# Half of the second MLP product by Strassen's seven block products, interleaved with the first product

## The chip, the cores and the metric

The kernel runs on one core of one Trainium2 chip. Its time is the device time of one execution in microseconds, the median of several runs. A core has five engines that work through queues of their own and wait for each other by semaphores: TensorE (PE; its weight loads are listed as PEld), VectorE (DVE), ScalarE (ACT), GpSimd (POOL) and SyncE (SP, which here issues the loads of weights). The order in each queue is fixed when the program is built.

## The reference

One decoder layer on 256 tokens with 2048 features, all float32. Two token mixers (attention and a gated recurrence) come first; the part that matters here is the MLP at the end:

```
x = x + merged @ w_out
u = relu(rmsnorm(x) * g @ w_mlp1)      # w_mlp1: 2048 x 8192
return x + (u * u) @ w_mlp2            # w_mlp2: 8192 x 2048
```

## The kernel before, in words

Weights stream from HBM in tiles ("units") of 128 x 2048 float32, 1 MB each, 258 of them. Each is cut into two parts: ACT copies it to `hi` in the rounded type float32r, DVE subtracts to get the rest, `lo` = raw - hi. A product is then the sum of three: hi x hi, lo x hi, hi x lo. `unit()` hands out the next unit and, before it does, issues the load and the cut of the unit two further on; raw, `hi` and `lo` have three buffers each.

The MLP runs in four parts. A part makes 2048 of the 8192 hidden features and then adds what they contribute to the output:

- First product, 16 units of `w1` (`ws`, L288 and L290): features on partitions, 256 tokens in the columns. Each unit takes 16 matmuls of 512 columns (`hi` of the weight against both parts of x2) and 16 of 256 columns. Its result leaves PSUM in two pieces (`cross` on ACT, then an addition on DVE), goes through relu and the norm on DVE, is squared on ACT, and is cut into the parts of `ucat`, 128 x 256 each.
- Second product, 16 units of `w2` (L666 to L668): for each block b of 512 output columns, two PSUM banks (t = 0, 1, the two halves of the tokens) take 4 units. A unit is 4 rows of k by 2 values of t by 3 matmuls of 512 columns: 24. After the fourth unit the banks are copied by ACT (part 0) or added by DVE into `acc` (L674, L676).

At the end `turn` transposes the sums on PE, adds them to x2 and stores. x2 stays in SBUF from the layer's middle to the end. PSUM has eight banks, four in the pool `pmain` and four in `pside`. The scheduler that orders the queues keeps nearly the order of the code but moves instructions of one engine past each other where they don't depend.

The lines of the profile that follow: L116 makes `hi`, L117 makes `lo`, L301 `cross`, L302 the addition, L650 the relu with the norm, L652 the square, L314 and L315 the two parts of `ucat`, L612 the last addition into x2.

Of the kernel before, what the change touches and what calls it, by code (L numbers as in the profile page):

```python
# [9 lines left out]
F32 = mybir.dt.float32  # L10
# [6 lines left out]
P = 128  # L17
T = 256
# [12 lines left out]
def layer_kernel(ctx: ExitStack, tc: tile.TileContext, xT, vecs, wv, wm, wg, wu, wo, w1, w2, cf, cm, out):  # L31
# [3 lines left out]
    wp = ctx.enter_context(tc.tile_pool(name="weights", bufs=3))  # L35
    catp = ctx.enter_context(tc.tile_pool(name="cat", bufs=1))
    gp = ctx.enter_context(tc.tile_pool(name="gen", bufs=20))
    sp = ctx.enter_context(tc.tile_pool(name="small", bufs=3))
# [9 lines left out]
    def g4(s, shape=(P, 1024), dt=F32):  # L48
        return gp.tile(list(shape), dt, tag="g", name=uid(s))

    def s1(s, dt=F32, n=256):
        return sp.tile([P, n], dt, tag=f"s{n}", name=uid(s), bufs=6 if n == 256 else 3)

    def bank(s, pool=pp):
        return pool.tile([P, 512], F32, tag="b", name=uid(s))
# [13 lines left out]
    for p in range(4):  # L69
        for u in range(16):  # L70
            units.append(w1[16 * p + u])
        for b in range(4):
            at = 32 * (p // 2) + 8 * b
            w = w2[at : at + 8].rearrange("(u s) p f -> s p u f", s=2)[p % 2]
            for q in range(4):
                units.append(w[:, :, q * 512 : (q + 1) * 512])
# [9 lines left out]
    def load(u):  # L86
        if u >= len(units) or u in raws:
            return
        raws[u] = wp.tile([P, UW], F32, tag="raw", name=f"raw{u}")
        for s in pieces(u):  # L90
            if u < 4:
                load_x(u, s)
            if len(units[u].shape) == 2:
                nc.sync.dma_start(raws[u][:, s], units[u][:, s])
            else:
                nc.sync.dma_start(raws[u].rearrange("p (u f) -> p u f", u=4), units[u])
# [9 lines left out]

    def cut(u):
        if u >= len(units):
            return
        hi = wp.tile([P, UW], F32R, tag="hi", name=f"hi{u}")  # L110
        lo = wp.tile([P, UW], F32R, tag="lo", name=f"lo{u}")
        raw = raws[u]
# [8 lines left out]
    done = [0]  # L121

    def unit():
        u = done[0]
        done[0] += 1
        load(u + AHEAD)
        cut(u + AHEAD)
        return split.pop(u)
# [26 lines left out]
    warm = gp.tile([P, 512], F32R, tag="g", name="warm")  # L155
# [8 lines left out]
    cft = cp.tile([P, 128 + 256], F32, name="cft")  # L164
    rope = cp.tile([32, 512], F32, name="rope")
# [3 lines left out]
    def load_consts():  # L169
        nc.sync.dma_start(cft, cf[:, :384])  # L170
# [7 lines left out]
    ident = cft[:, :128]  # L178
    cmask = cft[:, 128:384]
# [36 lines left out]
    def prepare():  # L216
# [12 lines left out]
        ssum = cp.tile([P, T], F32, name="ssum")  # L229
# [93 lines left out]
    def recur(g, q, f):  # L323
# [36 lines left out]
        for lv in range(LEVELS):  # L360
# [3 lines left out]
            if lv < 7:  # L364
# [44 lines left out]
                nt = sp.tile([P, n], F32, tag="tot" if n > 256 else "tots", name=uid("tot"), bufs=2)  # L409
# [63 lines left out]
    def rotate(x):  # L473
        r = gp.tile([32, 4, T], F32, tag="g", name=uid("rot"))
# [7 lines left out]
    def attend(g, q, k):  # L482
# [8 lines left out]
        nmx = sp.tile([P, 8], F32, tag="c8", name=uid("nmx"), bufs=8)  # L491
        sm = sp.tile([P, 8], F32, tag="c8", name=uid("sm"), bufs=8)
# [107 lines left out]

    x2 = []
# [5 lines left out]
    acc2 = s1("acc2")  # L607
# [15 lines left out]
    rstd2 = cp.tile([P, T], F32, name="rstd2")  # L623


    x2cats = [x2cat[:, k, :] for k in range(KD)]
    acc = [[g4("acc", (P, 1024)) for _ in range(2)] for _ in range(2)]

    def turn(b):

        for j in range(4):
            ptr = bank("pt")
            for t in range(2):
                a = acc[t][b // 2][:, (b % 2) * 512 + j * P : (b % 2) * 512 + (j + 1) * P]
                nc.tensor.transpose(ptr[:, t * P : (t + 1) * P], a, ident)  # L635
            d = x2[b][:, j, :]
            nc.vector.tensor_add(d, ptr[:, :T], d)
            (nc.scalar if j % 2 else nc.sync).dma_start(out[4 * b + j], d)

    for part in range(4):  # L640
        ucat = []
        for j in range(16):
            pst = ws(unit_parts(*unit(), x2cats))
            if part == 0 and j == 0:
                ps2 = bank("ps_ss2")
                nc.tensor.matmul(ps2[:, :T], ones, acc2, start=True, stop=True)
                rms_rows(ps2[:, :T], rstd2, D)
            t = s1("t")
            summed(pst, t)
            nc.vector.scalar_tensor_tensor(t, t, 0.0, rstd2, op0=OP.max, op1=OP.mult)  # L650
            u2 = s1("u2")
            nc.scalar.activation(u2, t, AF.Square)  # L652
            if j % 2 == 0:
                ut = g4("ucat", (P, 2, 512), F32R)
            to_parts((ut[:, j % 2, :T], ut[:, j % 2, T:]), u2)
            ucat.append(ut[:, j % 2, :])
        for b in range(4):
            pst = [bank(f"py{t}", pm) for t in range(2)]
            for q in range(4):
                hi, lo = (w.rearrange("p (u k f) -> p k u f", u=4, k=4) for w in unit())  # L660
                for k in range(4):
                    kk = 4 * q + k
                    for t in range(2):
                        uh = ucat[kk][:, t * P : (t + 1) * P]
                        ul = ucat[kk][:, T + t * P : T + (t + 1) * P]
                        nc.tensor.matmul(pst[t], uh, hi[:, k], start=(kk == 0), stop=False)  # L666
                        nc.tensor.matmul(pst[t], uh, lo[:, k], start=False, stop=False)  # L667
                        nc.tensor.matmul(pst[t], ul, hi[:, k], start=False, stop=(kk == 15))  # L668
                if part == 3 and q == 0 and b > 0:
                    turn(b - 1)  # L670
            for t in range(2):
                d = acc[t][b // 2][:, (b % 2) * 512 : (b % 2 + 1) * 512]
                if part == 0:
                    nc.scalar.activation(d, pst[t], AF.Copy)  # L674
                else:
                    nc.vector.tensor_add(d, pst[t], d)  # L676
    turn(3)


# [84 lines left out]
```

## Time and profile before

| | us |
|---|---|
| median of 3 runs (lowest, highest) | 1431.89 (1430.42, 1432.04) |
| the profiled execution | 1432.35 |
| its span | 1430.6 |
| the MLP in it | about 718 to 1424 |

| engine | busy us | share |
|---|---|---|
| PE | 1423.7 | 100% |
| PEld | 1231.1 | 86% |
| DVE | 873.0 | 61% |
| ACT | 697.2 | 49% |

The busy time of PE is modelled from matmuls that overlap, so the spacing of matmuls is read from their starts. A mean over the span hides that the stages load DVE and ACT differently; the windows by stage show that.

### The profile page before, as it was taken

Reading aid. Unit: us, or ns where it says so; the run is one execution under the profiler, and the core shown is the slowest. Engines: PE = TensorE matmul, PEld = TensorE weight load, DVE = VectorE, ACT = ScalarE, POOL = GpSimd, SP = SyncE. Lnnn points to the kernel's source line nnn. Section 1 sums busy time; section 2 is a strip of 40 time slices with the busy share of each in tenths; the row PEclk is TensorE's granted clock in tenths of the full one; section 3 lists DMA queues with packets and bytes.
Section 4 is the critical chain, followed back from the end, with each engine's and each line's share of the span. In section 5 each row is a group of like instructions: output and inputs, shape, how many; then the busy total and the mean of one; then the engine's idle time right before and its main releaser. Section 6 shows DMA issues by size and latency. Waiting matters only on the chain.

```text
span 1430.6 us, 19881 instructions
## 1 busy us (share of the span) xinstructions
PE 1423.7 (100%) x8400; PEld 1231.1 (86%) x8400; DVE 873.0 (61%) x956; ACT 697.2 (49%) x794; POOL 4.9 (0%) x12
## 2 busy tenths in 40 slices
PE   9999999999999999999999999999999999999998
PEld 7888888888888888888888888888888888888887
DVE  7445776667876676666666534565546654566553
ACT  7444444676655555544454443554334543344431
POOL 0000000000000000000000000000000000000000
PEclk9999999999999999999999999999999999999999
DMA  8655544444443555555455565555665556555671
GB/s 302 226 200 193 177 158 160 156 177 177 177 147 148 193 205 208 204 194 203 178 192 190 178 188 196 204 182 183 194 204 191 194 177 193 190 206 180 185 222 61
DMA packets 67081, 267.99 MB, mean 187 GB/s; under 512 B 5648, under 2 KB 7824, under 8 KB 44208
## 3 DMA queue, kind: packets, MB, share of 16 engines
q1 hardware_dynamic: 65120, 263.53, 53.4%
q0 software_dynamic: 576, 2.10, 0.4%
q8 instruction: 66, 1.08, 0.3%
q10 hardware_dynamic: 1296, 1.09, 0.2%
q14 instruction: 23, 0.19, 0.0%
HBM read 264.60 MB, written 2.10 MB: 186 GB/s over the span
## 4 chain that ended last, share of the span: by engine, by line
PE 99%; DMA 0%; DVE 0%; ACT 0%; issue 0%; DVEq 0%
PE pw L288 43%; PE pw L290 22%; PE py L667 8%; PE py L666 8%; PE py L668 8%; PE pv L271 2%; PE pv L272 2%; PE pv L273 2%; PE pd L373 0%; PE pl L504 0%; DMA vt<-vecs 0%; PE pt L635 0%; PE pd L380 0%; PE pb L448 0%; PE pb L449 0%; PE ptr L526 0%
## 5 line engine op out<-in xcount | busy, mean ns | idle before, releaser
L117 DVE TENSOR_TENSOR lo<-raw,hi 128x2048 fp32r<-128x2048 f32 (+2 forms) x258 | 569.0, 2207 | 454.9 <-ACT hi L116 453.4
L116 ACT ACTIVATE hi<-raw 128x2048 fp32r<-128x2048 f32 (+2 forms) x258 | 475.5, 1845 | 444.0 <-PE pw L288 200.2
L288 PE MATMUL pw<-xcat,hi 128*128 128x512 f32 x1152 | 278.1, 393 | 0.0
L288 PEld LDWEIGHTS pw<-xcat,hi 128*128 128x128 f32 x1152 | 212.0, 188 | 42.2
L288 PE MATMUL pw<-x2cat,hi 128*128 128x512 f32 x1024 | 244.4, 391 | 0.0
L288 PEld LDWEIGHTS pw<-x2cat,hi 128*128 128x128 f32 x1024 | 188.5, 188 | 36.8 <-DVE x2cat L614 0.2
L666 PE MATMUL py<-hi,ucat 128*128 128x512 f32 x512 | 199.5, 390 | 0.0
L667 PE MATMUL py<-lo,ucat 128*128 128x512 f32 x512 | 199.2, 389 | 0.0
L668 PE MATMUL py<-hi,ucat 128*128 128x512 f32 x512 | 199.2, 389 | 0.0
L290 PEld LDWEIGHTS pw<-xcat,lo 128*128 128x128 f32 x1152 | 147.7, 191 | 5.6
L290 PE MATMUL pw<-xcat,lo 128*128 128x256 f32 x1152 | 149.4, 283 | 0.0
L290 PEld LDWEIGHTS pw<-x2cat,lo 128*128 128x128 f32 x1024 | 131.3, 191 | 4.9
L290 PE MATMUL pw<-x2cat,lo 128*128 128x256 f32 x1024 | 132.8, 283 | 0.0
L668 PEld LDWEIGHTS py<-hi,ucat 128*128 128x128 f32 x512 | 96.1, 188 | 20.0
L666 PEld LDWEIGHTS py<-hi,ucat 128*128 128x128 f32 x512 | 96.2, 188 | 19.8
L667 PEld LDWEIGHTS py<-lo,ucat 128*128 128x128 f32 x512 | 96.2, 188 | 19.6
L652 ACT ACTIVATE u<-t 128x256 f32<-128x256 f32 x64 | 26.4, 412 | 131.6 <-DVE t L650 131.6
L301 ACT ACTIVATE cross<-pw 128x256 f32<-128x256 f32 x168 | 62.2, 371 | 35.9 <-PE pw L290 35.8
L288 PE MATMUL pw<-mcat,hi 128*128 128x512 f32 x256 | 61.2, 391 | 0.0
L288 PEld LDWEIGHTS pw<-mcat,hi 128*128 128x128 f32 x256 | 47.0, 188 | 9.4 <-DVE mcat L315 0.3
L271 PE MATMUL pv<-hi,xcat 128*128 128x512 f32 x128 | 50.1, 399 | 1.2 <-ACT xcat L200 1.2
L272 PE MATMUL pv<-lo,xcat 128*128 128x512 f32 x128 | 50.5, 395 | 0.0
(172 smaller groups left out, 994.3 us busy)
## 6 DMA issues: line engine op xcount, KB each, us to landing
raw<-w SPq DMA_DIRECT2D x128, 1024.0 KB, 5.5
raw<-wm SPq DMA_DIRECT2D x56, 1024.0 KB, 4.8
raw<-wg SPq DMA_DIRECT2D x16, 1024.0 KB, 4.8
raw<-wu SPq DMA_DIRECT2D x16, 1024.0 KB, 4.8
raw<-wo SPq DMA_DIRECT2D x16, 1024.0 KB, 4.8
raw<-wv SPq DMA_DIRECT2D x10, 1024.0 KB, 4.9
raw<-wv SPq DMA_DIRECT2D x8, 512.0 KB, 7.2
raw<-wv SPq DMA_DIRECT2D x8, 256.0 KB, 5.5
```

Source lines behind the costliest of these rows:

```text
L116: nc.scalar.activation(hi[:, s], raw[:, s], AF.Copy)
L117: nc.vector.tensor_sub(lo[:, s], raw[:, s], hi[:, s].bitcast(F32))
L271: nc.tensor.matmul(pst[t], xh, hi[:, k, :], start=(kk == 0), stop=False)
L272: nc.tensor.matmul(pst[t], xh, lo[:, k, :], start=False, stop=False)
L273: nc.tensor.matmul(pst[t], xl, hi[:, k, :], start=False, stop=(kk == KD - 1))
L288: nc.tensor.matmul(pst, h, cat, start=(i == 0), stop=False)
L290: nc.tensor.matmul(pst[:, T:], l, cat[:, :T], start=False, stop=(i == n - 1))
L301: nc.scalar.activation(c, pst[:, T:], AF.Copy)
L652: nc.scalar.activation(u2, t, AF.Square)
L666: nc.tensor.matmul(pst[t], uh, hi[:, k], start=(kk == 0), stop=False)
L667: nc.tensor.matmul(pst[t], uh, lo[:, k], start=False, stop=False)
L668: nc.tensor.matmul(pst[t], ul, hi[:, k], start=False, stop=(kk == 15))
```

## The change

The hidden features are now taken in eight eighths of 1024. For the output columns of b = 0 and 1, a pair of values of t and the two halves of an eighth form 2 x 2 blocks, and seven of the eight eighths compute them by Strassen's scheme in Winograd's form: seven block products instead of eight, each 4 x 3 matmuls of 512 columns. The columns of b = 2 and 3 stay plain and gather in four PSUM banks (`slow`) over all eighths. Each of the seven products is added into its own SBUF tile (`fast`), and `combine` forms the four blocks once at the end. The sums of u (`side_sums`) and the differences of weights (`p_t1` to `p_t4`) are made on DVE. While an eighth's second product runs, the first product of the next one runs in between, in the order of a string of 19 letters: f a unit of the first product, s one of the seven, p a plain unit. The last eighth is done plainly. x2 is written to HBM before the MLP and read back at the end, and the pools of the early stages are closed and replaced.

```diff
+    dp = ctx.enter_context(tc.tile_pool(name="spill", bufs=1, space=bass.MemoryType.DRAM))
...
+    early = ExitStack()
+    pool = {
+        "g": early.enter_context(tc.tile_pool(name="gen", bufs=20)),
+        "s": early.enter_context(tc.tile_pool(name="small", bufs=3)),
+    }
...
+    def rows(k, b):
+        half, s, q = k // 8, k // 4 % 2, k % 4
+        at = 32 * half + 8 * b
+        w = w2[at : at + 8].rearrange("(u s) p f -> s p u f", s=2)[s]
+        return w[:, :, q * 512 : (q + 1) * 512]
...
+    def ahead(u):
+        if u < MLP:
+            load(u)
+            cut(u)
+        elif u - MLP < len(later):
+            split[u] = later[u - MLP][0]()
...
+    slow = [[bank(f"py{b}{t}") for t in range(2)] for b in range(2)]
...
+    def raw_of(name, src):
+        if name[0] == "w":
+            r = wp.tile([P, UW], F32, tag="raw", name=uid(name))
+        else:
+            r = pool["s"].tile([P, UW], F32, tag="raw2", name=uid(name), bufs=2)
+        if len(src.shape) == 2:
+            nc.sync.dma_start(r, src)
+        else:
+            nc.sync.dma_start(r.rearrange("p (u f) -> p u f", u=4), src)
+        return r
...
+    def halves(r):
+        hi, lo = two_parts(uid("w"))
+        nc.scalar.activation(hi, r, AF.Copy)
+        nc.vector.tensor_sub(lo, r, hi.bitcast(F32))
+        return hi, lo
...
+            if j == 0:
+                ucat[c] = []
+                usum[c] = [g4("uk", (P, 4, T)) for _ in range(2)]
+            pst = ws(unit_parts(*unit(), x2cats))
...
+            if j == 7 and c + 1 < EIGHTHS:
+                side_sums(c)
...
+    def side_sums(c):
+        (a1, a2), H = usum.pop(c), slice(0, P)
+        L = slice(P, T)
+        nc.vector.tensor_add(a2[:, :, L], a1[:, :, L], a2[:, :, L])
+        nc.vector.tensor_sub(a1[:, :, L], a1[:, :, H], a1[:, :, L])
+        nc.vector.tensor_sub(a1[:, :, H], a2[:, :, L], a1[:, :, H])
+        nc.vector.tensor_sub(a2[:, :, H], a2[:, :, H], a1[:, :, H])
+        parts = []
+        for a in (a1, a2):
+            h, l = (g4(n, (P, 4, T), F32R) for n in ("sh", "sl"))
+            to_parts((h, l), a)
+            parts.append((h, l))
+        upart[c] = parts
...
+    def rows_product(pst, stat, parts, begin, end):
+        hi, lo = (w.rearrange("p (u k f) -> p k u f", u=4, k=4) for w in parts)
+        for k, (xh, xl) in enumerate(stat):
+            nc.tensor.matmul(pst, xh, hi[:, k], start=(begin and k == 0), stop=False)
+            nc.tensor.matmul(pst, xh, lo[:, k], start=False, stop=False)
+            nc.tensor.matmul(pst, xl, hi[:, k], start=False, stop=(end and k == 3))
...
+            for t in range(2):
+                rows_product(banks[t], of_u(c, half, t), parts, begin, end)
...
+    def seven(c):
+        w = {}
...
+        def p_b11():
+            w["b11"] = raw_of("b11", rows(2 * c, 0))
+            return halves(w["b11"])
...
+        def p_t1():
+            w["b12"] = raw_of("b12", rows(2 * c, 1))
+            nc.vector.tensor_sub(w["b11"], w["b12"], w["b11"])
+            return halves(w["b11"])
+        def p_t3():
+            w["b22"] = raw_of("w22", rows(2 * c + 1, 1))
+            nc.vector.tensor_sub(w["b12"], w["b22"], w["b12"])
+            return halves(w["b12"])
+        def p_b22():
+            return halves(w["b22"])
+        def p_t2():
+            nc.vector.tensor_sub(w["b11"], w["b22"], w["b11"])
+            return halves(w["b11"])
+        def p_b21():
+            w["b21"] = raw_of("b21", rows(2 * c + 1, 0))
+            return halves(w["b21"])
+        def p_t4():
+            nc.vector.tensor_sub(w["b11"], w["b11"], w["b21"])
+            return halves(w["b11"])
...
+        def product(i, stat):
+            def run():
+                pst = bank(f"ps{i}", pm)
+                rows_product(pst, stat(), unit(), True, True)
+                if not fast:
+                    fast.extend(pool["s"].tile([P, 512], F32, tag="r", name=f"r{n}", bufs=7) for n in range(7))
+                r = fast[i - 1]
+                if c == 0:
+                    nc.scalar.activation(r, pst, AF.Copy)
+                else:
+                    nc.vector.tensor_add(r, pst, r)
+            return run
+        return [
+            (p_b11, product(1, lambda: of_u(c, 0, 0))),
+            (p_t1, product(5, lambda: of_sum(c, 1, 1))),
+            (p_t3, product(7, lambda: of_sum(c, 0, 1))),
+            (p_b22, product(3, lambda: of_sum(c, 1, 0))),
+            (p_t2, product(6, lambda: of_sum(c, 0, 0))),
+            (p_b21, product(2, lambda: of_u(c, 1, 0))),
+            (p_t4, product(4, lambda: of_u(c, 1, 1))),
+        ]
...
+    def combine():
+        r1, r2, r3, r4, r5, r6, r7 = fast
+        nc.vector.tensor_add(r6, r1, r6)
+        nc.vector.tensor_add(r1, r1, r2)
+        nc.vector.tensor_add(r3, r3, r5)
+        nc.vector.tensor_add(r3, r3, r6)
+        nc.vector.tensor_add(r7, r7, r6)
+        nc.vector.tensor_sub(r4, r7, r4)
+        nc.vector.tensor_add(r5, r7, r5)
...
+            if n == 0 and h == 0:
+                combine()
+                for i in range(4):
+                    t = g4("x2", (P, 4, T))
+                    nc.gpsimd.dma_start(t, kept[i])
+                    back.append(t)
+            if h == 1:
+                gather(b, ends[b])
+            elif n > 0:
+                turn(order[n - 1])
...
+    work = [first(0, j) for j in range(8)]
+    for c in range(LAST):
+        f = [first(c + 1, j) for j in range(8)]
+        s7 = seven(c)
+        pl = [plain(c, 2 + b, h, slow[b], c == 0 and h == 0, False) for b in range(2) for h in range(2)]
+        for name in "fsfpsfsfpsfsfpsfsfp":
+            work.append({"f": f, "s": s7, "p": pl}[name].pop(0))
+    work += [closing(n, h) for n in range(4) for h in range(2)]
...
+    kept = dp.tile([4, P, 4, T], F32, name="kept")
+    x2cats.extend(x2cat[:, k, :] for k in range(KD))
+    for c in range(4):
+        nc.gpsimd.dma_start(kept[c], x2[c])
+    early.close()
+    pool["g"] = ctx.enter_context(tc.tile_pool(name="gen2", bufs=15))
+    pool["s"] = ctx.enter_context(tc.tile_pool(name="small2", bufs=3))
+    for _, run in work:
+        run()
+    turn(order[-1])
```

Two engines' queues in a stretch where the MLP is in its steady run. VectorE (DVE) before, from the end of a part's second product into the next part's first: `lo` is the cut, `acc` the eviction of the second product, `t` and `ucat` the way of a first-product result.

```order
L117 TENSOR_TENSOR lo185_8977<-raw185_8974,hi185_8976 128x2048
L676 TENSOR_TENSOR acc_533_6455<-py0_695_8882,acc_533_6455 128x512
L676 TENSOR_TENSOR acc_535_6457<-py1_696_8883,acc_535_6457 128x512
L117 TENSOR_TENSOR lo186_9009<-raw186_9006,hi186_9008 128x2048
L117 TENSOR_TENSOR lo187_9058<-raw187_9055,hi187_9057 128x2048
L302 TENSOR_TENSOR t_698_9045<-pw_697_9012,cross_699_9046 128x256
L650 SCALAR_TENSOR_TENSOR t_698_9045<-t_698_9045,rstd2_6453 128x256
L315 TENSOR_TENSOR ucat_701_9052<-u2_700_9050,ucat_701_9052 128x256
L117 TENSOR_TENSOR lo188_9106<-raw188_9103,hi188_9105 128x2048
```

VectorE in the changed kernel, from the beginning of an eighth to its third Strassen product: `low` is the cut, `w1` a tile of the first weight, `b11`, `b12`, `w22` tiles of the second, `sl` the cut of a sum of u, `r0` and `r4` evictions of Strassen products.

```order
L328 TENSOR_TENSOR sl_814_8797<-uk_743_8182,sh_813_8796 128x1024
L328 TENSOR_TENSOR sl_816_8801<-uk_744_8183,sh_815_8800 128x1024
L328 TENSOR_TENSOR ucat_826_8881<-uk_819_8834,ucat_826_8881 128x256
L760 TENSOR_TENSOR r0_6940<-ps1_827_8884,r0_6940 128x512
L638 TENSOR_TENSOR low_831_8908<-b11_817_8804,hiw_831_8907 128x2048
L315 TENSOR_TENSOR t_833_8944<-pw_832_8911,cross_834_8945 128x256
L638 TENSOR_TENSOR low_836_8955<-w1_835_8952,hiw_836_8954 128x2048
L658 SCALAR_TENSOR_TENSOR t_833_8944<-t_833_8944,rstd_164 128x256
L732 TENSOR_TENSOR b12_830_8904<-w22_838_8983,b12_830_8904 128x2048
L328 TENSOR_TENSOR ucat_826_8881<-uk_819_8834,ucat_826_8881 128x256
L739 TENSOR_TENSOR b11_817_8804<-w22_838_8983,b11_817_8804 128x2048
L638 TENSOR_TENSOR low_839_8987<-b12_830_8904,hiw_839_8986 128x2048
```

Between the cuts there now stand the differences of weights (L732, L739), the cuts of sums and the evictions of single products, and the steps of one first-product result are spread among them.

ScalarE (ACT) before, at the start of a part's first product:

```order
L116 ACTIVATE hi185_8976<-raw185_8974 128x2048
L116 ACTIVATE hi186_9008<-raw186_9006 128x2048
L116 ACTIVATE hi187_9057<-raw187_9055 128x2048
L301 ACTIVATE cross_699_9046<-pw_697_9012 128x256
L652 ACTIVATE u2_700_9050<-t_698_9045 128x256
L314 ACTIVATE ucat_701_9052<-u2_700_9050 128x256
L116 ACTIVATE hi188_9105<-raw188_9103 128x2048
L301 ACTIVATE cross_704_9095<-pw_702_9061 128x256
L652 ACTIVATE u2_705_9099<-t_703_9094 128x256
L116 ACTIVATE hi189_9154<-raw189_9152 128x2048
```

ScalarE in the changed kernel, in the same stretch of an eighth as above:

```order
L637 ACTIVATE hiw_831_8907<-b11_817_8804 128x2048
L327 ACTIVATE sh_815_8800<-uk_744_8183 128x1024
L660 ACTIVATE uk_819_8834<-t_824_8875 128x256
L327 ACTIVATE ucat_826_8881<-uk_819_8834 128x256
L637 ACTIVATE hiw_836_8954<-w1_835_8952 128x2048
L314 ACTIVATE cross_834_8945<-pw_832_8911 128x256
L660 ACTIVATE uk_819_8834<-t_833_8944 128x256
L327 ACTIVATE ucat_826_8881<-uk_819_8834 128x256
L637 ACTIVATE hiw_839_8986<-b12_830_8904 128x2048
L637 ACTIVATE hiw_841_9005<-w1_840_9003 128x2048
L637 ACTIVATE hiw_848_9054<-w2_847_9052 128x2048
```

Here `hiw` of the difference `b12` (made by DVE's L732) has moved ahead of two further tiles, and what stands behind it in the queue waits with it.

## Rows read from the trace of the kernel before

**Rows 1.** Page, busy time by engine; PE clock in 40 slices

```profile
PE 1423.7 (100%) x8400; PEld 1231.1 (86%) x8400; DVE 873.0 (61%) x956; ACT 697.2 (49%) x794; POOL 4.9 (0%) x12
...
PEclk9999999999999999999999999999999999999999
```

**Rows 2.** Page, the chain that ended last, shares by engine

```profile
PE 99%; DMA 0%; DVE 0%; ACT 0%; issue 0%; DVEq 0%
```

**Rows 3.** Windows: the MLP; columns us, busy time (instructions) of each engine, PE clock, DMA

```profile
718.00:1424.00 706.00, 706.00 (x3605) 604.71 (x3604) 381.40 (x356) 304.42 (x329) 0.00 (x0) 1.00 0.56 186
```

**Rows 4.** Timeline, first product on PE: start, duration, engine, line, tile, count

```profile
910.55 3.82 PE L288 MATMUL pw<-x2cat,hi 128*128 128x512 f32 x16
...
914.20 2.08 PE L290 MATMUL pw<-x2cat,lo 128*128 128x256 f32 x16
...
916.12 3.82 PE L288 MATMUL pw<-x2cat,hi 128*128 128x512 f32 x16
```

**Rows 5.** Timeline, second product, 24 matmuls apart; then its end

```profile
850.36 0.39 PE L666 MATMUL py<-hi,ucat 128*128 128x512 f32 x1
...
855.80 0.39 PE L666 MATMUL py<-hi,ucat 128*128 128x512 f32 x1
...
893.65 0.39 PE L668 MATMUL py<-hi,ucat 128*128 128x512 f32 x1
893.88 3.79 PE L288 MATMUL pw<-x2cat,hi 128*128 128x512 f32 x16
```

**Rows 6.** Groups by line and shape: count, busy us, mean ns, idle before

```profile
L117 DVE TENSOR_TENSOR lo<-raw,hi 128x2048 fp32r<-128x2048 f32 x242 | 554.1, 2290 | 452.6 <-ACT hi L116 451.2 <-PE ptr L526 1.3
L116 ACT ACTIVATE hi<-raw 128x2048 fp32r<-128x2048 f32 x242 | 462.6, 1911 | 440.1 <-PE pw L288 200.2 <-PE py L668 190.3 <-issue 21.0
...
L676 DVE TENSOR_TENSOR acc<-py,acc 128x512 f32<-128x512 f32 x24 | 16.5, 691 | 17.9 <-PE py L668 17.9
...
L408 DVE TENSOR_TENSOR rqp<-rqp,tot 128x512 f32<-128x512 f32 x12 | 8.2, 682 | 0.0
...
L443 DVE TENSOR_TENSOR sql<-sq,sqh 128x1024 fp32r<-128x1024 f32 x6 | 7.3, 1218 | 3.1 <-ACT sqh L441 3.1
...
L441 ACT ACTIVATE sqh<-sq 128x1024 fp32r<-128x1024 f32 x6 | 6.3, 1054 | 0.1
```

**Rows 7.** Timeline, DVE and ACT in the first product

```profile
910.87 2.29 DVE L117 TENSOR_TENSOR lo<-raw,hi 128x2048 fp32r<-128x2048 f32 x1 [2.29 <-ACT hi L116]
...
913.08 0.42 DVE L315 TENSOR_TENSOR ucat<-u,ucat 128x256 fp32r<-128x256 f32 x1
913.41 0.42 DVE L302 TENSOR_TENSOR t<-pw,cross 128x256 f32<-128x256 f32 x1
913.86 0.43 DVE L650 SCALAR_TENSOR_TENSOR t<-t,rstd 128x256 f32<-128x256 f32 x1
...
914.32 0.42 ACT L652 ACTIVATE u<-t 128x256 f32<-128x256 f32 x1 [2.92 <-DVE t L650]
914.64 1.90 ACT L116 ACTIVATE hi<-raw 128x2048 fp32r<-128x2048 f32 x1
...
916.57 2.29 DVE L117 TENSOR_TENSOR lo<-raw,hi 128x2048 fp32r<-128x2048 f32 x1 [2.29 <-ACT hi L116]
916.75 0.37 ACT L301 ACTIVATE cross<-pw 128x256 f32<-128x256 f32 x1
```

**Rows 8.** Waits in the MLP: us in total, times, longest

```profile
DVE lo L117 <- ACT hi L116: 293.5, 125, 4.1
```

**Rows 9.** DMA issues: count, KB each, median us to landing

```profile
raw<-w SPq DMA_DIRECT2D x128, 1024.0 KB, 5.5
...
x<-xT POOLq DMA_DIRECT2D x4, 512.0 KB, 5.3
```

**Rows 10.** Timeline, DVE and ACT where the MLP begins

```profile
720.01 0.42 DVE L612 TENSOR_TENSOR x<-pw,x 128x256 f32<-128x256 f32 x1
...
723.98 0.38 ACT L301 ACTIVATE cross<-pw 128x256 f32<-128x256 f32 x1
```

More of the change, by code (lines that the diff above doesn't have):

```diff
@@ L68, in layer_kernel @@
         units.append(wo[u])
[L69 to L76, printed above, removed]
+    MLP = len(units)
+    def rows(k, b):
[3 more added lines that the diff above has]
+        return w[:, :, q * 512 : (q + 1) * 512]
     split = {}
@@ L105, in load_x, with two_parts @@
             nc.sync.dma_start(xr[c][:, k, :], xT[c][:, k, :])
+    def two_parts(u):
+        return [wp.tile([P, UW], F32R, tag=n, name=f"{n}{u}") for n in ("hi", "lo")]
     def cut(u):
@@ L125, in unit @@
         done[0] += 1
-        load(u + AHEAD)
-        cut(u + AHEAD)
+        ahead(u + AHEAD)
         return split.pop(u)
@@ new lines, in halves, with first, prep @@
+    def halves(r):
[3 more added lines that the diff above has]
+        return hi, lo
+    def first(c, j):
+        def prep():
+            return halves(raw_of("w1", w1[8 * c + j]))
+        def run():
[3 more added lines that the diff above has]
+            pst = ws(unit_parts(*unit(), x2cats))
+            if c == 0 and j == 0:
+                ps2 = bank("ps_ss2", pm)
+                nc.tensor.matmul(ps2[:, :T], ones, acc2, start=True, stop=True)
+                rms_rows(ps2[:, :T], rstd2, D)
+            t = s1("t")
+            summed(pst, t)
+            nc.vector.scalar_tensor_tensor(t, t, 0.0, rstd2, op0=OP.max, op1=OP.mult)
+            u2 = usum[c][j // 4][:, j % 4, :]
+            nc.scalar.activation(u2, t, AF.Square)
+            if j % 2 == 0:
+                ucat[c].append(g4("ucat", (P, 2, 512), F32R))
+            ut = ucat[c][j // 2]
+            to_parts((ut[:, j % 2, :T], ut[:, j % 2, T:]), u2)
+            if j == 7 and c + 1 < EIGHTHS:
+                side_sums(c)
+        return prep, run
@@ new lines, in plain, with prep, run @@
+    def plain(c, b, half, banks, begin, end):
+        def prep():
+            return halves(raw_of("w2", rows(2 * c + half, b)))
+        def run():
+            parts = unit()
+            for t in range(2):
+                rows_product(banks[t], of_u(c, half, t), parts, begin, end)
+        return prep, run
+    def seven(c):
[23 more added lines that the diff above has]
+        def product(i, stat):
+            def run():
+                pst = bank(f"ps{i}", pm)
[17 more added lines that the diff above has]
+        ]
@@ new lines, in layer_kernel @@
+    summed_up = [[None] * 4 for _ in range(2)]
+    def combine():
[7 more added lines that the diff above has]
+        nc.vector.tensor_add(r5, r7, r5)
+        summed_up[0][0], summed_up[0][1], summed_up[1][0], summed_up[1][1] = r1, r3, r4, r5
+    back = []
@@ new lines, in turn, with gather @@
+    def turn(b):
+        for j in range(4):
+            ptr = bank("pt", pm)
+            for t in range(2):
+                nc.tensor.transpose(ptr[:, t * P : (t + 1) * P], summed_up[t][b][:, j * P : (j + 1) * P], ident)
+            d = back[b][:, j, :]
+            nc.vector.tensor_add(d, ptr[:, :T], d)
+            (nc.scalar if j % 2 else nc.sync).dma_start(out[4 * b + j], d)
+    def gather(b, banks):
+        for t in range(2):
+            if b < 2:
+                d = summed_up[t][b]
+                nc.vector.tensor_add(d, banks[t], d)
+            else:
+                d = summed_up[t][b] = g4("acc", (P, 512))
+                nc.scalar.activation(d, banks[t], AF.Copy)
@@ new lines, in layer_kernel, with closing, run @@
+    LAST = EIGHTHS - 1
+    order = [2, 3, 0, 1]
+    ends = {2: slow[0], 3: slow[1]}
+    def closing(n, h):
+        b = order[n]
+        prep = plain(LAST, b, h, None, False, False)[0]
+        def run():
+            if h == 0 and b < 2:
+                ends[b] = [bank(f"pz{t}", pm) for t in range(2)]
+            parts = unit()
+            for t in range(2):
+                rows_product(ends[b][t], of_u(LAST, h, t), parts, h == 0 and b < 2, h == 1)
+            if n == 0 and h == 0:
[8 more added lines that the diff above has]
+                turn(order[n - 1])
+        return prep, run
@@ L622, in layer_kernel @@
             nc.vector.tensor_add(acc2, acc2, sq)
[L623 to L676, printed above, removed]
```

64 lines of the change are left out of this document (38 added, 26 removed).

## The prediction

> **What bounds the kernel now.** I read the summary first, then the chain that ended last, then the windows of the MLP, and last its timeline. The summary shows TensorE (PE) busy for the whole span at full clock, VectorE (DVE) 61% and ScalarE (ACT) 49% [rows 1]. The chain says the same from the other side: 99% of it is PE, nothing is a wait on another engine [rows 2]. In the MLP, from 718 us to 1424 us, PE has no gap at all and DVE is busy 381 of 706 us [rows 3]. So here time is the number of matmuls times their spacing, as long as the others keep PE supplied.
>
> The spacing: one unit of the first product (call it F) lasts 916.12 - 910.55 = 5.57 us; its 512-column half is over 3.65 us after its start and its 256-column half takes 1.92 us [rows 4]. One full unit of the second product (P), 24 matmuls of 512 columns, lasts 855.80 - 850.36 = 5.44 us, that is 0.2267 us a matmul [rows 5]. 64 of each make 705 us, which is the window.
>
> DVE's idle time there is nearly all one wait: the low half of a weight tile on ACT's high half, 293.5 us in 125 times [rows 8]. That is idleness of an engine which has been fast enough, and it is the only stock the change can draw on.
>
> **The change, part by part.**
>
> *Removed on PE.* In each of seven eighths, the columns b = 0 and 1 took 8 block products of 4 x 3 matmuls; now 7 (call such a half-length unit S: 12 x 0.2267 = 2.72 us). 12 matmuls x 7 = 84 fewer, as the orders also count. 84 x 0.2267 = **19.04 us**. The last eighth is done plainly, and the first product is unchanged.
>
> *Switches.* PE now changes kind of unit up to 126 times more often (18 in each of seven eighths). From below: the first F matmul after a P comes 0.23 us behind the last one, the ordinary spacing [rows 5], so 0. From above: within F, 3.65 us for 16 is 0.228 each and thus 0.02 us a unit over the P spacing [rows 4], so 126 x 0.02 = 2.5 us. I take 0, as the row of the switch itself says, and keep 2.5 for the range.
>
> *Added on DVE.* 19 tiles are cut per eighth instead of 16: 3 x 7 x 2.29 = 48.1 us. Four differences of weights per eighth, of the cut's size and types: 28 x 2.29 = 64.1. Sums of u: 28 x 0.68 = 19.1 and their cuts 14 x 1.22 = 17.1. Evictions: 46 additions instead of 24, so 22 x 0.69 = 15.2; the combining at the end 7 x 0.69 = 4.8 [rows 6]. Together 168 us on DVE. ACT gets 21 x 1.91 + 14 x 1.05 + 3 x 0.6 = 57 us (the 0.6 is an estimate from the 0.69 of DVE's eviction).
>
> Per steady eighth: PE 8 x 5.57 + 4 x 5.44 + 7 x 2.72 = **85.4 us** (88.1 before). DVE 19 x 2.29 + 4 x 2.29 + 8 x (0.42 + 0.42 + 0.42) + 7 x 0.69 + 4 x 0.68 + 2 x 1.22 = **73 us**. It fits on the average, with 12 us left. Averages don't settle it, since DVE and ACT run fixed queues and wait for each other; so I walked one eighth.
>
> *The walk.* Slots of an eighth are F S F P S F S F P S F S F P S F S F P, slot 0 at time 0; slots 1 to 8 start at 5.57, 8.29, 13.86, 19.30, 22.02, 27.59, 30.31 and 35.88. The tile of slot i goes into the buffers of slot i-3, so it can be cut only after that slot's end, which is the start of slot i-2. Spacings on DVE when nothing waits: 2.21 after a large cut, 0.33 or 0.45 after a small operation; an ACT result is used 0.03 us after its end [rows 7]; for the 512-wide ones I take duration less the same 0.08.
> - Cut of slot 1 (b11): buffer free at -5.1, runs -5.1 to -2.9. Addition, then the early difference t1 (-2.6 to -0.3), then F's scalar step, end 0.03. ACT squares, then makes the high half of slot 2 (0.4 to 2.3).
> - DVE: cut of slot 2 from 2.3; slot 17's u cut; first two sums of u to 6.3; slot 0's addition (its cross term is ready 0.38 us after slot 1's start plus 0.37, at 6.32, see the same offset at 916.12 and 916.75 [rows 4, 7]); the other sums, to 8.2.
> - Cut of slot 3 8.2 to 10.5 (needed 13.9: 3.4 spare). The two cuts of sums 10.4 to 12.7, u cut, eviction of slot 1 to 13.6.
> - Cut of t1 for slot 4 13.6 to 15.9 (needed 19.5: 3.6 spare). Cut of slot 5 to 18.4, difference t3 18.7 to 21.0, u cut, difference t2 21.3 to 23.5 while ACT makes t3's high half (21.1 to 23.0).
> - Cut of t3 for slot 6 23.5 to 25.8. Its second matmul wants it at 27.8: **2.0 us spare**, the smallest of the eighth.
> - From there it eases: slot 7 done at 28.5 (needed 34.0), slot 8 at 31.1 (36.1), slot 9 at 34.8 (41.5); after slot 9 only two differences are left, and DVE is waiting again.
>
> So every cut is there in time and the lost stock of idleness costs nothing; if this cover goes, slot 6 is late first. The t3 wait has behind it on DVE the eviction of slot 4 and the cuts of slots 7 and 8, and PE waits for each.
>
> *Loads.* 16 tiles per eighth as before. They wait in SP's queue for the low cut three tiles back, and behind the held tile w22 (free only after slot 9's cut). A load takes 5.5 us [rows 9]. By the walk slot 8's is issued at 18.4 behind slot 5's cut and lands at 23.9, wanted at 25.9; b21 holds SP until 25.8, then slot 10's lands some 34 us, wanted at 34 to 37 and needed at 44. No cost.
>
> *Set-up and end.* The new pools let the first cross term of the MLP wait until the last block of x2 is written out. The block's last addition ends at 720.43, the cross term ran at 723.98 [rows 10]; the write is not in this trace. Bounds: the 0.5 MB read by the same queue took 5.3 us [rows 9], so 725.7, 1.8 us late; from above, twice that, 731.0. I take the first. PE meets it only when slot 3 of the first eight F needs slot 0's bank: slot 1 began 0.38 before the cross term, slot 3 two F later, at 734.7. So it is hidden by 3 us at the least, and each us beyond would be one of PE. The reload of x2 is asked for while the last Strassen eighth runs, far ahead of its first use. The seven combining additions lie in DVE's queue in slots 12 to 18, where it has time. The last transposes, additions and stores are those of before.
>
> Sum against the profiled execution: 1432.35 - 19.04 = **1413.3 us** (span 1411.6). The median of the runs shown lies 0.5 lower, which I leave inside the range.
>
> **The rivals.**
>
> *A. Slot 6 late in every eighth.* If DVE needs more than 2.0 us more than in my walk from slot 17 to slot 6 (23 instructions), PE stops once an eighth. The same gap at the same place shows in the timeline. With 3 us: 1 us x 7, 1420; with 2.5: 1417. For it: the strided sums and differences were not timed in this place. Against it: all have a row of equal size.
> The Trainium skill (Perfetto Trace Analysis, Identifying Performance Opportunities) reads a gap that repeats on the engine that should be saturated as a sign that there is too little room for the next tile; three buffers for units half as long would be such a case. No gap of this kind is in the MLP of before.
>
> *B. DVE's queue takes over; slower.* The two engines hold each other up: ACT's squares wait for DVE, its next high half stands behind them, DVE's cut waits for that. In the trace DVE waits 2.29 us before a cut, and its cut starts right as ACT's ends [rows 7]. Harmless now; if in the crowded eighth such waits stay, the period becomes 73 us plus the waits. Place: the 8 cuts of F and the 4 of differences; point from which it decides: 15 us of waits in an eighth (88.1 - 73), that is 8 waits of 1.91. With 12: 73 + 22.9 = 95.9, 7.8 x 7 = 55 longer, 1487. For it: 293.5 us of such waits. Against it: they appear where DVE arrives early, and the walk finds 2 to 3 us of them up to slot 9.
> The Trainium skill (Perfetto Trace Analysis, Identifying the Most-Contended Engine) judges VectorE by occupancy and TensorE by weight loading: here 73 / 85.4 = 85% and 605 / 706 = 86% [rows 3], so by that page the two would be level after the change, and a shorter TensorE alone no sure gain. The trace has PE without a gap at 86%, so I hold with the gaps.
>
> *C. A single wait* at the new pools or the reload, 3 to 8 us in all: 1416 to 1421.
>
> **How the numbers follow.** Forecast 0.76 (own range 1411.5 to 1416, with the switches), A 0.11, B 0.08, C 0.05. All but B lie more than 0.2% (2.9 us, about what a measurement of this kernel can tell from no change) under the time of before. B in a weak form (15 us of waits) would be no change. So faster 0.91, same 0.03, slower 0.06. The range 1411.5 to 1421 takes in A and C and leaves out B.
>
> **What would show it.** PE: 84 matmuls fewer, F, P and S at 5.57, 5.44 and 2.72 us, no gap. DVE: busy about 168 us more. The cut of t3 ends about 2 us ahead of slot 6; if PE's wait stands there, A; if PE waits for many cuts and DVE still idles before cuts, B; a gap in the 30 us after the first F unit or at the first transposes of the end, C. A spacing of S well above 0.2267 a matmul would break the main term.

## The result, and the profile after

| | before | after |
|---|---|---|
| median, us (lowest, highest; 4 runs each) | 1431.18 (1430.42, 1432.04) | 1412.77 (1412.53, 1413.76) |
| ratio of the two, 95% interval | | 0.9873 [0.9855, 0.989] |
| the profiled execution, us | 1432.35 | 1412.66 |
| its span, us | 1430.6 | 1410.9 |

The forecast was 1413.3, and the kernel became 1.3% faster. The page of the changed kernel first: busy time, the clock in 40 slices, and the engines' shares of the chain that ended last.

```profile
PE 1402.8 (99%) x8316; PEld 1213.7 (86%) x8316; DVE 1024.4 (73%) x1076; ACT 763.6 (54%) x832; POOL 9.2 (1%) x20
...
PEclk9999999999999999999999999999999999999999
...
PE 99%; DVE 0%; DMA 0%; ACT 0%; issue 0%; DVEq 0%
```

PE has 84 instructions fewer than in [rows 1], the clock is full in every slice, and the chain is still PE's [rows 2]. The MLP as one window (columns as in [rows 3]; it ends earlier now, so the window does too):

```profile
718.00:1404.00 686.00, 685.31 (x3512) 587.02 (x3511) 531.67 (x477) 370.71 (x367) 2.65 (x5) 1.00 0.58 195
```

DVE has gone from 381 us of 706 to 532 of 686, and PE still has no more than 0.7 us of gaps. The waits (engine, line, who released it; us in total, times, longest) say what they are. These are the two of PE from 700 us to the end, and then DVE's wait that answers to [rows 8]:

```profile
PE pw L301 <- DVE x2cat L861: 0.7, 1, 0.7
PE pt L795 <- DVE r L804: 0.5, 1, 0.5
```

```profile
DVE low L638 <- ACT hiw L637: 123.9, 76, 4.5
```

PE's two single waits lie where x2 is finished and in the final transposes, not in an eighth. DVE's wait has shrunk from 293.5 us to 123.9, by 169.6: about 150 us of that is more busy time (381 to 532), about 20 us is that the window is shorter. So the new work was paid out of waiting.

### The profile page after: what moved, and what is told of

Same layout as the page of the kernel before. It is cut to its first block, busy times and chain, and to the rows that moved or that the text cites. A ratio compares the mean times of both kernels' runs of the same rounds, so it can differ in the third digit from the quotient of the medians.

```text
span 1410.9 us, 19868 instructions
## 1 busy us (share of the span) xinstructions
PE 1402.8 (99%) x8316; PEld 1213.7 (86%) x8316; DVE 1024.4 (73%) x1076; ACT 763.6 (54%) x832; POOL 9.2 (1%) x20
## 4 chain that ended last, share of the span: by engine, by line
PE 99%; DVE 0%; DMA 0%; ACT 0%; issue 0%; DVEq 0%
PE pw L301 43%; PE pw L303 23%; PE py L700 4%; PE py L701 4%; PE py L702 4%; PE ps L700 3%; PE ps L701 3%; PE ps L702 3%; PE pv L284 2%; PE pv L285 2%; PE pv L286 2%; PE pz L702 1%; PE pz L700 1%; PE pz L701 1%; PE pd L386 0%; PE pl L517 0%
## 5 line engine op out<-in xcount | busy, mean ns | idle before, releaser
L122 DVE TENSOR_TENSOR lo<-raw,hi 128x2048 fp32r<-128x2048 f32 (+2 forms) x130 | 275.7, 2125 | 160.5 <-ACT hi L121 159.1
L121 ACT ACTIVATE hi<-raw 128x2048 fp32r<-128x2048 f32 (+2 forms) x130 | 231.1, 1781 | 201.6 <-PE pw L301 150.3
L638 DVE TENSOR_TENSOR low<-w,hiw 128x2048 fp32r<-128x2048 f32 x107 | 244.8, 2288 | 83.9 <-ACT hiw L637 83.9
L637 ACT ACTIVATE hiw<-w 128x2048 fp32r<-128x2048 f32 x107 | 204.9, 1915 | 117.6 <-PE pw L301 49.9
L301 PE MATMUL pw<-x2cat,hiw 128*128 128x512 f32 x1024 | 243.2, 390 | 0.7 <-DVE x2cat L861 0.7
L301 PEld LDWEIGHTS pw<-x2cat,hiw 128*128 128x128 f32 x1024 | 191.7, 188 | 40.5 <-DVE x2cat L861 1.1
L303 PEld LDWEIGHTS pw<-x2cat,low 128*128 128x128 f32 x1024 | 131.3, 191 | 5.0
L303 PE MATMUL pw<-x2cat,low 128*128 128x256 f32 x1024 | 132.8, 283 | 0.0
L700 PE MATMUL py<-hiw,ucat 128*128 128x512 f32 x256 | 100.0, 391 | 0.0
L701 PE MATMUL py<-low,ucat 128*128 128x512 f32 x256 | 99.9, 390 | 0.0
L702 PE MATMUL py<-hiw,ucat 128*128 128x512 f32 x256 | 99.6, 389 | 0.0
```

The lines of the kernel that those rows point to most:

```text
L301: nc.tensor.matmul(pst, h, cat, start=(i == 0), stop=False)
L303: nc.tensor.matmul(pst[:, T:], l, cat[:, :T], start=False, stop=(i == n - 1))
L637: nc.scalar.activation(hi, r, AF.Copy)
L638: nc.vector.tensor_sub(lo, r, hi.bitcast(F32))
L700: nc.tensor.matmul(pst, xh, hi[:, k], start=(begin and k == 0), stop=False)
L701: nc.tensor.matmul(pst, xh, lo[:, k], start=False, stop=False)
```

## The experiments

Each one edits the changed kernel; "after" is that kernel's 1412.77 us. The kernel before, run beside the experiments, gave 1431.73 us (experiments 1 to 4) and 1430.63 us (5 to 7), and single runs of the kernel before lie up to 2 us apart; differences of medians under some 1.5 us are not read. Most of that scatter lies ahead of the MLP, in stages that the change leaves alone. So traces are also compared from one landmark, the start of ACT's last `x2cat` operation, to the end of the span; there the four kernels with the same matmuls (after and experiments 3, 5 and 6) lie at 692.1 to 692.2 us.

**1. Eight block products instead of seven.** The first of the seven is computed twice into its bank. Twelve matmuls come back in each of seven eighths; loads, cuts and sums stay.

```diff
-                rows_product(pst, stat(), unit(), True, True)
+                parts = unit()
+                for _ in range(2 if i == 1 else 1):
+                    rows_product(pst, stat(), parts, True, True)
```

> The changed kernel, but the first of the seven block products is computed twice (the second time over the first), so each of seven eighths has the 96 matmuls it had before the change, with all the rest of the change in place. Theory (the gain is 84 matmuls at 0.2267 us, the rest is hidden): 1412.8 + 19.0 = 1431.8, within 1 us of the kernel before. Rival (part of the gain comes from the new interleaving or from the end of the kernel): clearly below 1431. Rival (the added work of VectorE costs something that a longer product gives back): less than 19 us more than the changed kernel, for the same reason.

Measured: 1431.84 us (1431.39 to 1433.5, 11 runs), 1.0007 [0.9999, 1.0016] of before. Giving the 84 matmuls back costs 19.07 us by the medians; the main term of the forecast was 19.04. The landmark in the kernel before, in after and in this run:

```profile
720.46 0.51 ACT L613 ACTIVATE x2cat<-x,vt 128x256 fp32r<-128x256 f32 x1 [2.94 <-DVE x L612]
```

```profile
718.79 0.51 ACT L860 ACTIVATE x2cat<-x,vt 128x256 fp32r<-128x256 f32 x1 [2.95 <-DVE x L859]
```

```profile
720.53 0.51 ACT L862 ACTIVATE x2cat<-x,vt 128x256 fp32r<-128x256 f32 x1 [2.95 <-DVE x L861]
```

From there to the end of the span (1430.6, 1410.9 and 1431.7) it is 710.1, 692.1 and 711.2 us. So the 84 matmuls are worth 19.1 us, and all the rest of the rearrangement (interleaving, pools, DVE's work) costs 1.1. (The runs of this kernel lie as much above those of before: the lowest 1431.39 against 1430.31, the highest 1433.5 against 1432.43.) One part of it was found, PE's wait of 0.7 us for x2cat, shown above, which the kernel before does not have; the other 0.4 is not located.

**2. Two more DVE operations at the tightest place.** They stand behind the subtraction that forms t3, ahead of the cut for slot 6.

```diff
             nc.vector.tensor_sub(w["b12"], w["b22"], w["b12"])
+            nc.vector.tensor_max(w["b12"], w["b12"], w["b12"])
+            nc.vector.tensor_max(w["b12"], w["b12"], w["b12"])
```

> The changed kernel with two more VectorE operations of 128x2048 float32 (the maximum of the tile with itself, 2.2 us each) on the difference t3 before it is cut, in each of seven eighths: 4.4 us more of VectorE's time an eighth, where its average leaves 12 us free. Theory of the walk (2.0 us spare at slot 6; one eviction of 0.6 us has moved ahead of the cut as well): the cut of t3 comes 2.4 to 3.0 us late, TensorE waits that long once an eighth, 17 to 21 us in all: 1430 to 1434. Rival (only the average counts, or the spare time is larger than walked): 1413.

Measured: 1440.73 us (1437.37 to 1440.91, 5 runs), 28 us above after, 1.006 [1.0048, 1.0073] of before. The wait came where it was expected, and the price was higher than any of the sums. PE's waits in the MLP of this kernel, beside the two shown above:

```profile
PE pw L301 <- ACT hiw L637: 9.1, 7, 1.3
PE ps L700 <- ACT hiw L637: 5.9, 7, 2.6
```

15.0 us in all: 0.55 and 1.3 us in each of the seven eighths, and 2.1 more in the first. What PE waits for is ACT's high half of t3, and the next high half queued behind it. The profiled span is 26.6 us longer than that of after, so 15 us are not all of it. PE's timeline at one such place (start, duration, engine, line, tiles; in brackets the idle time before) shows what else is lost:

```profile
1147.35 0.50 PE L700 MATMUL ps<-hiw,sh 128*128 128x512 f32 x1 [0.55 <-ACT hiw L637]
1149.15 1.98 PE L301 MATMUL pw<-x2cat,hiw 128*128 128x512 f32 x4 [1.30 <-ACT hiw L637]
1150.93 0.63 PE L701 MATMUL ps<-low,sh 128*128 128x512 f32 x1
1151.36 0.63 PE L702 MATMUL ps<-hiw,sl 128*128 128x512 f32 x1
...
1152.90 0.40 PE L700 MATMUL ps<-hiw,sh 128*128 128x512 f32 x1
1153.14 0.40 PE L701 MATMUL ps<-low,sh 128*128 128x512 f32 x1
```

and the same stretch in windows (the column after POOL is PE's granted clock):

```profile
1147.00:1150.00 3.00, 1.35 (x3) 0.93 (x4) 3.00 (x3) 3.00 (x4) 0.00 (x0) 0.88 0.00 0
1150.00:1153.00 3.00, 3.00 (x9) 2.29 (x8) 3.00 (x3) 1.17 (x1) 0.00 (x0) 0.55 0.59 162
1153.00:1157.00 4.00, 4.00 (x19) 3.28 (x18) 2.94 (x4) 2.48 (x3) 0.00 (x0) 1.00 1.05 349
```

After the two stops, in a stretch where PE was busy 1.35 of 3 us, the granted clock is 0.55 for 3 us, which is near the lower of its two levels (1.2 of 2.4 GHz). Nine matmuls, from 1149.15 to 1152.90, take 3.75 us.

The clock did not fall behind each of these stops. They are as long in the third eighth, and there it stayed full:

```profile
970.31 0.50 PE L700 MATMUL ps<-hiw,sh 128*128 128x512 f32 x1 [0.55 <-ACT hiw L637]
972.11 1.19 PE L301 MATMUL pw<-x2cat,hiw 128*128 128x512 f32 x4 [1.29 <-ACT hiw L637]
...
974.28 0.39 PE L700 MATMUL ps<-hiw,sh 128*128 128x512 f32 x1
```

```profile
970.00:973.00 3.00, 1.39 (x5) 0.95 (x6) 3.00 (x3) 3.00 (x4) 0.00 (x0) 1.00 0.00 0
973.00:976.00 3.00, 3.00 (x15) 2.47 (x14) 3.00 (x3) 1.29 (x2) 0.00 (x0) 1.00 0.68 171
```

The nine matmuls from 972.11 to 974.28 take 2.17 us, so the lower clock costs 1.6. It came in five eighths of this execution and not in the third and the sixth. From one eighth's first stop to the next one's it is accordingly 89.3 us (1147.35 to 1236.69) or 87.7 (970.31 to 1058.03), against 85.33 in after: the two stops themselves cost 2.4 us, more than the 1.85 listed as idle. A wait is counted as idle only from the modelled end of the matmul before it, and that lies behind the place where the next one would ordinarily start (0.39 us long, 0.2267 apart). Seven times 2.4, 2.1 more in the first eighth and five times 1.6 make 26.9, the whole of the 26.6. What decides whether the clock falls behind such a stop is not shown.

The Trainium skill (Perfetto Trace Analysis, Identifying Performance Opportunities, under Optimization Strategy) says that a gap which repeats on the engine that should be saturated can come from too few buffers for the next tile. Here is such a gap, seven times; but its releaser is ACT's high half of a tile that stood behind DVE's queue, and no buffer was taken away to bring it about. So this trace gives another cause for such a gap; whether one more buffer would have closed it was not run.

**3. The same two operations on another tile.** They stand where b21 has been loaded, the tile used in slot 14.

```diff
             w["b21"] = raw_of("b21", rows(2 * c + 1, 0))
+            nc.vector.tensor_max(w["b21"], w["b21"], w["b21"])
+            nc.vector.tensor_max(w["b21"], w["b21"], w["b21"])
```

> The same two extra operations an eighth, but on the tile b21, which is cut for slot 14; they fall behind slot 6's cut, where the walk has 4 to 6 us spare. Theory: no change, 1412.8 (within 1 us), although VectorE is as busy as in the kernel with the two extra operations at t3. Rival (VectorE's load as such begins to cost, wherever it lies): as much as there, 17 us or more.

Measured: 1413.87 us (1412.41 to 1414.4, 4 runs), 0.9877 [0.9864, 0.9891] of before, and no new wait of PE. From the landmark (720.46) to the end (1412.6) it is 692.1 us, as in after. DVE's busy time is 1053.6 us, with the operations at t3 it was 1055.5. The same load costs 28 us at one place and nothing that can be told at another: the place decides, not the sum.

**4. The same units in sequence.** Only the order string changes.

```diff
-        for name in "fsfpsfsfpsfsfpsfsfp":
+        for name in "sssssssppppffffffff":
```

> The changed kernel with the order of each eighth as the seven products, then the four plain units, then the eight units of the next first product; same work, not interleaved. Theory (the queues decide, not the average): in the run of seven VectorE has about 34 us of work (7 cuts, 4 differences, 7 evictions, the sums of u) against 19 us on TensorE, less some 4 us that can be done ahead, and waits for the high halves on top: 10 to 20 us late an eighth, 1480 to 1550. Rival (the average decides: 73 of 85.4 us): 1413.

Measured: 1530.93 us (1529.43 to 1532.35, 4 runs), 1.0693 [1.0677, 1.0709] of before and 118 us over after. PE's waits in the MLP:

```profile
PE ps L700 <- ACT sh L327: 70.7, 7, 10.5
PE ps L700 <- ACT hiw L637: 8.5, 7, 1.3
PE py L700 <- ACT hiw L637: 7.8, 6, 1.3
```

87 us are waits, 71 of them once an eighth for the first cut of the sums of u. Most of the remaining 31 is the clock, which is at 0.94 as a mean of this MLP: adding up how much further apart than usual PE's matmuls start gives 91 us at the waits and 26 us in the stretches with the lower clock. The seven products without the first product between them lose six times what they save.

**5. One more operation at t3.** As experiment 2, with one line instead of two.

> One extra VectorE operation of 2.29 us (not two) behind the subtraction that forms t3, in each of the seven eighths. The walk puts the end of t3's low half 2.29 us later, 0.3 to 0.8 us behind the end of slot 6's first matmul group; TensorE's order puts three matmuls of the next slot there, which cover 0.68 us. So slot 6 stands 0 to 0.1 us an eighth. Theory (the walk: a place has its own spare time, 2.0 us here, and only what goes beyond it is paid): 1412.8 to 1414. Rival 1 (any stop, however short, lets the clock fall as after two extra operations, 1.7 us an eighth): 1425 or more. Rival 2 (VectorE's added time counts as such, half of what two operations cost): about 1427.

Measured: 1414.15 us (1413.99 to 1414.25, 4 runs), 0.9883 [0.9869, 0.9898] of before; no new wait of PE, clock 1.00 in the MLP. From the landmark (720.19) to the end (1412.4) it is 692.2 us, in after 692.1. DVE's cut of t3 and PE's slot 6, in one eighth:

```profile
1130.51 2.29 DVE L638 TENSOR_TENSOR low<-b,hiw 128x2048 fp32r<-128x2048 f32 x1
```

```profile
1131.94 0.40 PE L700 MATMUL ps<-hiw,sh 128*128 128x512 f32 x1
1132.17 1.09 PE L301 MATMUL pw<-x2cat,hiw 128*128 128x512 f32 x4
1133.10 0.39 PE L701 MATMUL ps<-low,sh 128*128 128x512 f32 x1
```

The low half is ready at 1132.80, 0.63 us after slot 6 would have wanted it (its second matmul would have followed at 1132.17). In PE's order four matmuls of the next first-product unit stand there, and they cover 0.93 us. So the step from no cost to cost lies between one and two such operations, where the walk and those matmuls together have it, and not in proportion to DVE's load (half of experiment 2's 28 us would have been 1427). As PE did not stop, whether a shorter stop lets the clock fall stays open.

**6. No differences of weights.** The four `tensor_sub` in `p_t1`, `p_t3`, `p_t2` and `p_t4` are taken out.

```diff
-            nc.vector.tensor_sub(w["b11"], w["b12"], w["b11"])
...
-            nc.vector.tensor_sub(w["b12"], w["b22"], w["b12"])
...
-            nc.vector.tensor_sub(w["b11"], w["b22"], w["b11"])
...
-            nc.vector.tensor_sub(w["b11"], w["b11"], w["b21"])
```

> The four differences of blocks of weights (28 VectorE operations of 2.29 us, 64 us in all) are left out, so that four of the seven block products are formed with plain blocks; TensorE's 8316 matmuls, the loads and the sums of u stay. Theory (all of VectorE's added work lies beside TensorE): 1412.8, unchanged within 0.2%. Rival (some of it still ends on the path, for instance at the start of each eighth): faster, down to the 1402.8 us of TensorE's busy time plus about 2, some 1405 to 1410.

Measured: 1413.29 us (1412.38 to 1414.15, 4 runs), 0.9876 [0.9859, 0.9892] of before: the time of after. From the landmark (719.95) to the end (1412.1) it is 692.2 us, in after 692.1. The window of the MLP:

```profile
718.00:1404.00 686.00, 685.31 (x3512) 586.91 (x3511) 479.15 (x449) 372.48 (x367) 2.65 (x5) 1.00 0.59 195
```

DVE is busy 52.5 us less and PE exactly as long. This is the plainest evidence that the differences, the largest part of DVE's added work (64 of 168 us), are hidden. It also decides on the second rule cited in the prediction: the Trainium skill (Perfetto Trace Analysis, Identifying the Most-Contended Engine) has VectorE judged by occupancy and TensorE by weight loading (and by its share of peak arithmetic, not worked out here), which in after's MLP are 532 / 686 = 78% and 587 / 686 = 86%. (The 85% worked out for VectorE was for a steady eighth and counted overlaps twice; there it measures 69 of 85.3 us, 81%.) By that rule TensorE is the one to shorten, which agrees with the result; the 14% that it leaves open on TensorE are not there to be had, since the matmuls follow each other without a gap.

**7. The last eighth by seven products too.** It saves 12 more matmuls, but no first product is left to stand between them.

```diff
-    work += [closing(n, h) for n in range(4) for h in range(2)]
+    s7 = seven(LAST)
...
+    pl = [closing(b, h) for b in (2, 3) for h in range(2)]
+    for name in "spsspsspssp":
+        work.append({"s": s7, "p": pl}[name].pop(0))
...
-    turn(order[-1])
+    for b in (0, 1, 3):
+        turn(b)
```

> The last eighth of the second product goes by seven block products as well, behind the interleaved ones, where no first product of a next eighth is left to stand between them. 12 matmuls fewer: 2.72 us less TensorE work. Theory (without units of the first product between them, the block products wait for their cuts): VectorE has about 47 us of sums, differences and cuts beside 40.8 us of TensorE there, the sums of u come before the first product that needs them (10.5 us wait an eighth where the products ran in sequence), and two more of the four output turns stand at the very end: 1416 to 1430. Rival (only the count of matmuls matters): 1410.1.

Measured: 1415.95 us (1414.65 to 1417.12, 4 runs), 0.9896 [0.9881, 0.991] of before. It is not faster than after, as a count of matmuls alone would have it (1410.1); it lies at the lower edge of what was expected. One stop stands in its last eighth:

```profile
1368.98 0.73 PE L700 MATMUL py<-hiw,ucat 128*128 128x512 f32 x2 [2.00 <-ACT hiw L637]
1369.94 0.50 PE L700 MATMUL ps<-hiw,sh 128*128 128x512 f32 x1 [0.22 <-ACT sh L327]
...
1374.40 0.39 PE L700 MATMUL ps<-hiw,sh 128*128 128x512 f32 x1
```

```profile
1372.00:1374.00 2.00, 2.00 (x6) 1.59 (x5) 2.00 (x2) 0.00 (x0) 0.00 (x0) 0.50 0.05 19
```

The clock is at 0.50 behind the stop, and the 12 matmuls from 1369.94 to 1374.40 take 4.46 us instead of 2.72. With 2.0 us of stop and two waits of 0.2, that is 4.1 us against a saving of 2.72. The rest is the end of the kernel, first of this one, then of after:

```profile
1405.39 2.33 PE L795 MATMUL pt<-ident,r 128*128 128x128 f32 x16
1407.71 1.34 PE L795 MATMUL pt<-ident,acc 128*128 128x128 f32 x8
```

```profile
1405.27 0.49 PE L795 MATMUL pt<-ident,r 128*128 128x128 f32 x3
1406.22 0.76 PE L795 MATMUL pt<-ident,r 128*128 128x128 f32 x5 [0.46 <-DVE r L804]
```

Reckoned from the landmark (718.55 here, 718.79 in after), the last transposes begin 0.4 us later than in after, although 16 of those that after had done before are still to come: 24 stand at the end instead of 8, and from there to the end of the span it is 7.8 us (1413.2 - 1405.4) against 5.6. The sum of the terms ahead of that place is about -0.6: -2.7, +4.1, and about -2 for the 16 transposes (eight of them lengthen a stretch of after's matmuls by 1.0 us). +0.4 was measured; that 1 us is not accounted for. The expected long wait for the sums of u hardly came (0.2 us); in this order plain units stand between the products, in experiment 4 none did.

## Why the prediction was right, point by point

*The main term.* 84 matmuls at 0.2267 us, 19.04; putting them back costs 19.07 by the medians and 19.1 from the landmark (experiment 1). The whole change gained less: 18.4 by the medians, 18.0 from the landmark. (The 19.7 between the two profiled executions hold 1.7 us that lie ahead of the landmark.) So the sum misses a cost of 1.1 us, and it started from the profiled execution of before, 1432.35, which lies 1.2 above the median; from the median it gives 1412.1. That the forecast came within 0.5 us of 1412.77 is in part luck, since the two cancel. The mechanism does not hang on it.

*Switches at nothing.* DVE's timeline repeats after 85.33 us in a steady eighth (one operation at 1089.39 us, its like at 1174.72); the working had 85.4. With the upper bound of 0.02 us for 18 switches it would have been 85.7. The lower bound, which I took, holds within the 0.4 us that experiment 1 leaves unlocated.

*The walk.* Slot 0 of this eighth begins on PE at 1102.89, slot 1 at 1108.42. Two lines of PE for that, then three of DVE and two of PE at slot 6:

```profile
1102.89 2.43 PE L301 MATMUL pw<-x2cat,hiw 128*128 128x512 f32 x10
...
1108.42 0.40 PE L700 MATMUL ps<-hiw,ucat 128*128 128x512 f32 x1
```

```profile
1121.47 2.29 DVE L732 TENSOR_TENSOR b<-w,b 128x2048 f32<-128x2048 f32 x1
...
1124.01 2.29 DVE L739 TENSOR_TENSOR b<-w,b 128x2048 f32<-128x2048 f32 x1
1126.21 2.29 DVE L638 TENSOR_TENSOR low<-b,hiw 128x2048 fp32r<-128x2048 f32 x1
```

```profile
1130.44 0.40 PE L700 MATMUL ps<-hiw,sh 128*128 128x512 f32 x1
1130.67 0.40 PE L701 MATMUL ps<-low,sh 128*128 128x512 f32 x1
```

From slot 0, t3's difference begins at 18.6 (walk 18.7), t2's at 21.1 (21.3), the cut of t3 runs from 23.3 to 25.6 (23.5 to 25.8). The second matmul of slot 6 wants it at 1130.67, 2.2 us later; the walk had 2.0. Three of DVE's durations were taken from other shapes or places, and none was off by more than 0.01 us. One reading was wrong without harm: the walk has slot 0's cross term start 0.38 us behind slot 1, but the two rows that it names are 0.63 apart (916.12 and 916.75); here it is 0.20 (1108.62). That this place has little to spare, and slot 14 more, is shown by experiments 2, 3 and 5; that it has the least of all is argued by the walk alone.

*DVE's 168 us.* As a sum of durations it stands: DVE's operations add up to 913 us before and 1081 after. The page shows only 151.4 more (1024.4 - 873.0), because operations that follow each other at once overlap by some 0.08 us in the trace and busy time counts that once. ACT's busy time rose by 66.4 us where 57 were worked out. By durations it is 59 (the groups of ACT in the MLP add up to 322 us before and 381 after); the rest is that fewer of its operations overlap now, 10 us in place of 17.

*Loads.* Their landing was mis-sized: 6.1 and 6.2 us where I took the 5.5 of [rows 9] (DMA issues; count, KB each, median us to landing):

```profile
w<-w SPq DMA_DIRECT2D x107, 1024.0 KB, 6.1
...
b<-w SPq DMA_DIRECT2D x21, 1024.0 KB, 6.2
```

In the waits of the MLP there is also one that the walk did not have, ACT's high half for a load:

```profile
ACT hiw L637 <- DMA w<-w: 15.1, 6, 3.1
```

Six times, 3.1 us at most, and none reaches PE. The conclusion (no cost) held, with less room than the working gave it.

*Set-up.* The first cross term came 4.8 us late, waiting for x2 to be written out; the bounds were 1.8 and about 7, I took the lower one. ACT's line and PE's units behind it:

```profile
727.11 0.39 ACT L314 ACTIVATE cross<-pw 128x256 f32<-128x256 f32 x1 [4.79 <-DMA kept<-x]
```

```profile
728.13 3.82 PE L301 MATMUL pw<-x2cat,hiw 128*128 128x512 f32 x16
...
733.69 3.82 PE L301 MATMUL pw<-x2cat,hiw 128*128 128x512 f32 x16
...
739.26 2.91 PE L301 MATMUL pw<-x2cat,hiw 128*128 128x512 f32 x12
```

PE's units follow each other at 5.56 and 5.57 us, so it is hidden, as worked out.

*The rivals.* A (slot 6 late) and C (a single wait of 3 to 8 us) are not in the trace; PE's two single waits are 0.7 and 0.5 us. B (DVE's queue takes over) is not either: DVE's waits are what is left of its old stock. Experiment 2 shows that A was priced too low: it reckoned with the stop alone. A stop listed with 1.85 us of idle time cost 2.4, and 4.0 where the clock fell behind it. Had slot 6 been late by as much, the time would have been above the range given.

## What to carry to other kernels

Where TensorE has no gap, a change is worth the matmuls that it takes away, and the work that it adds elsewhere is free as long as every operand arrives ahead of the matmul that reads it; to know that, walk one period of the fixed queues with durations from the trace, because busy shares don't tell it (the same 4.6 us of VectorE work an eighth cost 28 us at one place and nothing at another). Interleave a stage whose operands are dear with one whose operands are cheap: the same units in sequence lost 118 us. And price a stop of TensorE by the time from one period to the next, since its listed length leaves out part of it and the clock that can fall behind it. Where single executions differ ahead of the changed part, compare them from a landmark at its start.

## What was not expected of the hardware

In experiment 2 a stop of TensorE (0.55 and 1.3 us of idle time with one matmul between, in the first eighth 2.6 and 1.3) was followed by a lower clock in five of seven eighths of one execution; in the other two, behind 0.55 and 1.3 us as well, the clock stayed full. In the place shown where it fell, the granted clock was 0.55 over the next 3 us (0.50 over 2 us in the last eighth of experiment 7) and the spacing 0.43 us in place of 0.2267, which added 1.6 us. In experiment 5, where other matmuls filled the place and PE did not stop, the clock stayed at 1.00.
